# Longer hand-written issue order ahead of attention, and a later start for the pool and LRU branches

## The chip, the cores and the metric

The kernel runs on one core of one Trainium2 chip. The metric is the device time of one execution in microseconds (us); lower is better. Inside a core five engines work beside each other, each with its own instruction queue that is worked off in order: PE (TensorE, matrix products), DVE (VectorE), ACT (ScalarE), POOL (GpSimd) and SP (SyncE, which issues the DMAs here).

## What is computed

Two layers of a hybrid decoder on a sequence of 512 positions with 1024 channels, in float32. Each layer has a mixing part with three parallel branches, merged by sigmoid gates, and a squared-ReLU MLP:

```python
for l in range(DEPTH):                      # 2
    h = rms_norm(x, g_mix[l])
    proj = h @ w_in[l]
    u_pool, q_lat, kv_lat, u_lru, gate_logit = jnp.split(proj, [...], axis=-1)
    y_pool = pool_mixer(u_pool, w_pool_grp[l], pool_scale[l]) @ w_pool_proj[l]
    y_mla = mla_mixer(q_lat, kv_lat, ...) @ w_mla_o[l]      # 8 heads, causal
    y_lru = rg_lru_mixer(u_lru, conv_w[l], ...) @ w_lru_proj[l]
    gates = jax.nn.sigmoid(gate_logit + b_gate[l]).reshape(B, S, N_BRANCH, D)
    merged = gates[:, :, 0] * y_pool + gates[:, :, 1] * y_mla + gates[:, :, 2] * y_lru
    x = x + merged @ w_out[l]
    h = rms_norm(x, g_ffn[l])
    x = x + jnp.square(jax.nn.relu(h @ w_ff1[l])) @ w_ff2[l]
return rms_norm(x, g_final)
```

`pool_mixer` takes causal means over windows of 2, 4, 8 and 16 positions, minus the input, and multiplies each group by a small matrix. `rg_lru_mixer` is a causal convolution of width 4, two small gate products, and a linear recurrence along the sequence.

## The kernel before, in words

Activations lie with channels on the 128 partitions and the 512 positions along the free dimension. Every matrix product is made to float32 accuracy from three products of a high and a low part (`three`): `hi·hi`, `hi·lo`, `lo·hi`. So each weight block of 128x1024 that SP loads (`raw`) is split by ACT (`whi`, a cast, L139) and by DVE (`wlo`, a subtraction, L140); `chunk` does all of that. Two such split blocks and three raw ones fit at a time (`N_W` = 2, `N_RAW` = 3). Activations are split in the same way (`split`, L156 and L157: ACT the high part, DVE or POOL the remainder). `acc` gives one of three PSUM accumulators of 512 columns; a product can begin only when one has been read out.

The mixing part of a layer runs through `mixer` and `merge`:

1. The input projections: the latents for keys and queries, the two LRU blocks and the two pool blocks. This stretch stands in `with tc.manual_schedule(engines=ORDERED)`: inside it PE, DVE and ACT keep the order in which the code is written. It ends with `prefetch(C_V)`, `conv(1)` (the second block's convolution, one multiply at L350 and three multiply-adds at L353, on DVE) and `scaled(project(C_POOL + 1), pm[1])` (L314: DVE reads the last projection out of its accumulator).
2. Outside that block a planner sets the order. It runs a simulation of the engines while it lists instructions: an engine takes, of what is ready, the instruction that comes first in the code. So what is written far behind can be placed early, wherever the simulation sees an engine free. This holds for `windows(0)` and `windows(1)` (the sums of the pool branch on DVE, L364 to L371), for the four products `va` that give the attention's values, and for all that follows.
3. Attention: eight heads, each with score products `s`, a softmax on DVE and ACT (L518 to L524), transposes `t` (L530) and output products `o` (L538). At the heads named in `EARLY` a `gate` is issued: 24 products of 512 columns into `ga`, a multiplication by `rstd` on DVE (L286), a tanh on ACT (L287). There are 24 gates in a layer, three for each of eight output blocks; they keep PE supplied while DVE and ACT work on the softmax.
4. `merge` runs over the 24 gates. At gate `LRU_N` it writes `pool_lru_out`: for each of the two blocks a split of the LRU input and of the pool sums, small products `ra` and `pa`, and a chain of activations up to the recurrence (L571) and a last split. Ahead of that, in layer 0 alone, `setup_vectors` computes small per-channel constants (L260 to L279) that the branch needs. After gate 14 the first merging product `pj` needs the results of all three branches; gates and the convolved LRU inputs share `N_X` = 15 buffers.

`with tc.issue_after(ins)` puts the instructions of its block behind `ins` on the engine of `ins`; `last_gate` holds the last gate's DVE multiplication.

Of the kernel before, what the change touches and what calls it, by code (L numbers as in the profile page):

```python
# [10 lines left out]
F32R = mybir.dt.float32r  # L11
# [4 lines left out]
P = 128  # L16
D = 1024
S = 512
# [16 lines left out]
N_BUSY = 10  # L35
HEAD = 10
SPLIT = 4
EARLY = (0, 2, 4, 6)
LRU_N = 9
DEPTH = 4  # L40
ON_POOL = 2
ORDERED = {mybir.EngineType.PE, mybir.EngineType.DVE, mybir.EngineType.Activation}
# [24 lines left out]
def trunk(ctx: ExitStack, tc, x_in, wts, vecs, consts, out):  # L67
# [66 lines left out]
    def chunk(l, c, cols=1024, off=0):  # L134
        if (l, c) in ready:
            return ready.pop((l, c))
        raw = load(l, c, cols, off)
        hi, lo = wtiles(l, c)
        nc.scalar.copy(hi[:, :cols], raw[:, :cols])  # L139
        nc.vector.tensor_tensor(lo[:, :cols], raw[:, :cols], f(hi[:, :cols]), op=ALU.subtract)  # L140
        return hi, lo
# [139 lines left out]
    def gate(l, rstd, xs, n):  # L281
        j, b = divmod(n, 3)
        a = acc(f"ga{l}_{j}{b}")
        dense(a, chunk(l, C_MIX + 4 * j + b), xs)
        g = xtile(f"g{l}_{j}{b}")
        last_gate[:] = [nc.vector.tensor_tensor(g, a, rstd, op=ALU.mult).ins]  # L286
        nc.scalar.activation(g, g, AF.Tanh, bias=hb[:, l, 4 + 8 * b + j:5 + 8 * b + j], scale=0.5)  # L287
        return g

    def mixer(l, mix, rstd, xs):  # L290
# [3 lines left out]
        with ExitStack() as st:  # L294
# [61 lines left out]
            def windows(b):  # L356

                z, sums = pm[b], []
                cur = z
                for w in (1, 2) if b == 0 else (1, 2, 4, 8):  # L360

                    r = slice(0, P) if len(sums) + 1 < (2 if b == 0 else 4) else slice(64, P)
                    t = xtile(f"win{l}_{b}{w}")
                    nc.vector.tensor_copy(t[r, :w], cur[r, :w])  # L364
                    nc.vector.tensor_tensor(t[r, w:], cur[r, w:], cur[r, :S - w], op=ALU.add)
                    sums.append(t)
                    cur = t
                for r, t in ((slice(0, 64), sums[-2]), (slice(64, P), sums[-1])):
                    cnt = cst[r, K_CNT + 16 * b:K_CNT + 16 * b + 16]
                    nc.vector.tensor_tensor(t[r, 0:16], t[r, 0:16], cnt, op=ALU.mult)  # L370
                    nc.vector.scalar_tensor_tensor(z[r], t[r], cst[r, K_INV + b:K_INV + b + 1], z[r],  # L371
                                                   op0=ALU.mult, op1=ALU.subtract)
# [7 lines left out]
            with tc.manual_schedule(engines=ORDERED):  # L380
# [75 lines left out]
                prefetch(C_V)  # L456
                conv(1)
                scaled(project(C_POOL + 1), pm[1])
            for b in range(2):
                windows(b)  # L460


            wv = chunk(l, C_V)
            v = []
            for t in range(4):
                a = acc(f"va{l}_{t}")
                terms = []
                for k in range(2):
                    h, lo = ckv[k]
                    terms += three(blk(h, t), blk(lo, t), wv[0][:, k * S:(k + 1) * S], wv[1][:, k * S:(k + 1) * S])  # L470
                matmuls(a, terms)
                vv = at.tile([P, NH, 2, DV], F32R, tag="v", bufs=4, name=f"v{l}_{t}")
                split(a.rearrange("p (h d) -> p h d", h=NH), vv[:, :, 0, :], vv[:, :, 1, :])
                v.append(vv)

            pt = [at.tile([P, 13, P], F32R, name=f"pt{l}{c}") for c in "hl"]
            for t in pt:
                nc.vector.memset(f(t[:, 11, :]), 0.0)

            early = []  # L480
            for h in range(NH):
                if h in EARLY:
                    early.append(gate(l, rstd, xs, len(early)))
                e, pr = h % 2, h // 2
# [62 lines left out]
    def pool_lru_out(l, mix, us, pm):  # L547
        w = chunk(l, C_SMALL, 768)
        res = [], []
        for b in range(2):  # L550
            py, ly = (tuple(mix.tile([P, S], F32R, tag="lat", bufs=10, name=f"{n}{c}{l}_{b}") for c in "hl") for n in ("py", "ly"))
            res[0].append(py)
            res[1].append(ly)
            u = us[b]
            split(u, *ly)
            tr, ti = tmp(f"tr{l}_{b}"), tmp(f"ti{l}_{b}")
            for g, t in enumerate((tr, ti)):
                a = acc(f"ra{l}_{b}{g}")
                dense(a, w, [ly], 2 * b + g)
                nc.scalar.activation(t, a, AF.Tanh, bias=hb[:, l, 2 * g + b:2 * g + b + 1], scale=0.5)  # L560

            av, th = tmp(f"av{l}_{b}"), tmp(f"th{l}_{b}")
            sc, ns = sp4[:, l, b:b + 1], nsp4[:, l, b:b + 1]
            nc.scalar.activation(av, tr, AF.Exp, bias=ns, scale=ns)
            nc.scalar.activation(th, tr, AF.Tanh, bias=sc, scale=sc)
            nc.scalar.activation(tr, av, AF.Square)
            nc.vector.scalar_tensor_tensor(th, tr, 1.0, th, op0=ALU.add, op1=ALU.mult)
            nc.scalar.activation(th, th, AF.Sqrt, scale=0.25)
            nc.vector.scalar_tensor_tensor(ti, ti, 1.0, u, op0=ALU.add, op1=ALU.mult)
            nc.vector.tensor_tensor(th, th, ti, op=ALU.mult)  # L570
            nc.vector.tensor_tensor_scan(u, av, th, 0.0, op0=ALU.mult, op1=ALU.add)  # L571
            split(u, *ly)
            split(pm[b], *py)
            a = acc(f"pa{l}_{b}")
            dense(a, w, [py], 4 + b)
            split(a, *py, vcol(l, V_PSC + b))
        return res

    def merge(l, mix, mg, rstd, xs, us, pm, ot, early):
        def project(j, gates):  # L580
            w = chunk(l, C_MIX + 4 * j + 3)
            for b, br, off in ((0, py, 0), (2, ly, 6), (1, ot, 2)):
                a = acc(f"pj{l}_{j}{b}")
                dense(a, w, br, off)
                nc.vector.scalar_tensor_tensor(gates[b], gates[b], 1.0, a, op0=ALU.add, op1=ALU.mult)
                if b:
                    eng = nc.vector if j == KB - 1 else nc.gpsimd
                    eng.tensor_tensor(gates[0], gates[0], gates[b], op=ALU.add)
            h = mg.tile([P, S], F32R, tag="mgh", bufs=KB, name=f"mgh{l}_{j}")
            lo = mg.tile([P, S], F32R, tag="mgl", bufs=KB, name=f"mgl{l}_{j}")  # L590
            split(gates[0], h, lo, 0.5)
            return h, lo

        res = []
        gates = list(early)
        for n in range(3 * KB):
            if n == LRU_N:
                py, ly = pool_lru_out(l, mix, us, pm)
            if n >= len(early):
                gates.append(gate(l, rstd, xs, n))  # L600
            if l == 0 and n == len(early):
                with tc.issue_after(last_gate[0]):
                    setup_vectors()
            j = n // 3 - DEPTH
            if n % 3 == 2 and j >= 0:
                res.append(project(j, gates[3 * j:3 * j + 3]))
        for j in range(KB - DEPTH, KB):
            res.append(project(j, gates[3 * j:3 * j + 3]))
        return res
# [252 lines left out]
```

## Time and profile before

| | us |
|---|---|
| median of 3 runs | 1406.41 (1405.29 to 1406.43) |
| profiled execution, its time | 1406.01 |
| its span, first to last instruction | 1404.1 |
| PE busy | 1382.6 (98% of the span) |
| DVE busy | 780.1 (56%) |
| ACT busy | 559.6 (40%) |
| POOL busy | 257.8 (18%) |

PE is busy nearly throughout, so what is left lies in the few stretches where it waits. Times in rows are counted from the start of the span. Layer 0's mixing part takes about 0 to 352 us, its MLP 352 to 700; layer 1 follows from 700 with the same pattern.

### The profile page before, as it was taken

The numbers are of one execution on the slowest core, as the hardware profiler recorded it, in microseconds if no ns is written. First come the engines' busy times: TensorE is split into PE (matmuls) and PEld (weight loads), VectorE is DVE, ScalarE is ACT, GpSimd is POOL, SyncE is SP. The second block draws the span as 40 slices with busy tenths as digits, with TensorE's granted clock in tenths as the row PEclk, the third lists the DMA queues.
The fourth block names the chain that finished last, engine by engine and source line by source line (L and its number), as shares of the span: only waits on it lengthen the run. The fifth ranks groups of instructions, "written<-read, shape, count | busy, mean of one in ns | idle before, by whom it ended". The sixth has DMA issues, their size and how long they took to land.

```text
span 1404.1 us, 16125 instructions
## 1 busy us (share of the span) xinstructions
PE 1382.6 (98%) x6262; PEld 1145.4 (82%) x6262; DVE 780.1 (56%) x1174; ACT 559.6 (40%) x849; POOL 257.8 (18%) x181
## 2 busy tenths in 40 slices
PE   9999999999999999999999999999999999999997
PEld 7787888888888888888887878888888888888886
DVE  6998875475544324443369987655745433344323
ACT  6467683324422113232344777632343221222322
POOL 0025101033221002211100530111222200022112
PEclk9999999999999999999999999999999999999998
DMA  6221223343333332333332211223423333323231
GB/s 222 88 76 55 68 79 91 102 153 97 99 91 104 90 105 91 100 103 117 123 99 84 77 61 64 91 90 109 147 90 105 93 103 91 104 90 105 91 102 63
DMA packets 42124, 137.38 MB, mean 98 GB/s; under 512 B 4672, under 2 KB 6848, under 8 KB 42048
## 3 DMA queue, kind: packets, MB, share of 16 engines
q1 hardware_dynamic: 41328, 135.76, 30.9%
q8 instruction: 49, 0.80, 0.2%
q10 hardware_dynamic: 720, 0.59, 0.1%
q14 instruction: 27, 0.22, 0.0%
HBM read 132.14 MB, written 4.19 MB: 97 GB/s over the span
## 4 chain that ended last, share of the span: by engine, by line
PE 89%; DVE 7%; ACT 2%; issue 1%; DMA 0%; SPq 0%; DVEq 0%; ACTq 0%
PE f L118 50%; PE ga L118 18%; PE wo L118 6%; PE pj L118 6%; PE in L118 2%; PE s L118 1%; DVE wlo L140 1%; PE o L538 1%; PE t L530 1%; PE qr L118 1%; PE qn L118 1%; PE ka L118 1%; DVE cu L353 1%; DVE p L524 0%; DMA raw<-wts 0%
## 5 line engine op out<-in xcount | busy, mean ns | idle before, releaser
L139 ACT CAST whi<-raw 128x1024 fp32r<-128x1024 f32 (+1 forms) x236 | 246.6, 1045 | 685.1 <-issue 383.2
L140 DVE TENSOR_TENSOR wlo<-raw,whi 128x1024 fp32r<-128x1024 f32 (+1 forms) x236 | 304.0, 1288 | 163.5 <-ACT whi L139 163.5
L118 PE MATMUL f<-al,whi 128*128 128x512 f32 (+1 forms) x528 | 202.2, 383 | 0.0
L118 PE MATMUL f<-ah,whi 128*128 128x512 f32 (+1 forms) x528 | 202.0, 383 | 0.0
L118 PE MATMUL f<-ah,wlo 128*128 128x512 f32 (+1 forms) x528 | 202.0, 383 | 0.0
L118 PE MATMUL f<-xhf,whi 128*128 128x512 f32 x512 | 199.2, 389 | 0.0
L118 PE MATMUL f<-xlf,whi 128*128 128x512 f32 x512 | 199.2, 389 | 0.0
L118 PE MATMUL f<-xhf,wlo 128*128 128x512 f32 x512 | 199.2, 389 | 0.0
L715 POOL TENSOR_TENSOR ft<-ft 128x512 f32<-128x512 f32 x64 | 94.7, 1481 | 426.6 <-ACT ah L714 426.6
L118 PE MATMUL ga<-xhm,whi 128*128 128x512 f32 x384 | 151.8, 395 | 3.1 <-ACT q L501 2.5
L118 PE MATMUL ga<-xhm,wlo 128*128 128x512 f32 x384 | 151.8, 395 | 0.0
L118 PE MATMUL ga<-xlm,whi 128*128 128x512 f32 x384 | 151.2, 394 | 0.0
L118 PEld LDWEIGHTS f<-al,whi 128*128 128x128 f32 x528 | 99.2, 188 | 19.5
L118 PEld LDWEIGHTS f<-ah,whi 128*128 128x128 f32 x528 | 99.2, 188 | 19.4
L118 PEld LDWEIGHTS f<-ah,wlo 128*128 128x128 f32 x528 | 99.2, 188 | 19.3
L118 PEld LDWEIGHTS f<-xlf,whi 128*128 128x128 f32 x512 | 96.1, 188 | 20.0
L118 PEld LDWEIGHTS f<-xhf,whi 128*128 128x128 f32 x512 | 96.1, 188 | 20.0
L118 PEld LDWEIGHTS f<-xhf,wlo 128*128 128x128 f32 x512 | 96.1, 188 | 19.9
L711 DVE SCALAR_TENSOR_TENSOR ft<-f,rstdf 128x512 f32<-128x512 f32 x64 | 44.1, 691 | 102.1 <-PE f L118 102.1
L118 PEld LDWEIGHTS ga<-xhm,whi 128*128 128x128 f32 x384 | 72.8, 189 | 18.2 <-ACT q L501 3.0
L118 PEld LDWEIGHTS ga<-xlm,whi 128*128 128x128 f32 x384 | 72.6, 189 | 14.6
L118 PEld LDWEIGHTS ga<-xhm,wlo 128*128 128x128 f32 x384 | 72.6, 189 | 14.3
(366 smaller groups left out, 2072.4 us busy)
## 6 DMA issues: line engine op xcount, KB each, us to landing
raw<-wts SPq DMA_DIRECT2D x232, 512.0 KB, 3.5
x<-x_in SPq DMA_DIRECT2D x8, 256.0 KB, 5.3
xr<-x_in SPq DMA_DIRECT2D x8, 256.0 KB, 3.1
saved<-xr SPq DMA_DIRECT2D x8, 256.0 KB, 2.0
xr<-saved SPq DMA_DIRECT2D x8, 256.0 KB, 2.8
out<-xr SPq DMA_DIRECT2D x12, 128.0 KB, 1.8
raw<-wts SPq DMA_DIRECT2D x4, 320.0 KB, 2.9
raw<-wts SPq DMA_DIRECT2D x4, 256.0 KB, 5.0
```

The lines of the kernel that those rows point to most:

```text
L118: ins = nc.tensor.matmul(dst, lhsT=a, rhs=b, start=(start and i == 0), stop=(stop and i == n - 1))
L139: nc.scalar.copy(hi[:, :cols], raw[:, :cols])
L140: nc.vector.tensor_tensor(lo[:, :cols], raw[:, :cols], f(hi[:, :cols]), op=ALU.subtract)
L353: nc.vector.scalar_tensor_tensor(u[:, o:], z[:, :S - o], cw(j), u[:, o:], op0=ALU.mult, op1=ALU.add)
L530: nc.tensor.transpose(tp[:, j, :], blk(probs[i], j), ident)
L538: nc.tensor.matmul(o[:, q0 * P:], lhsT=v[j][:, h, :, :], rhs=pt[c][:, 3 * j + q0:3 * j + 4, :], start=(j == 0 and c == 0), stop=(j == 3 an ...
L711: nc.vector.scalar_tensor_tensor(t, a, 0.0, rstd, op0=ALU.max, op1=ALU.mult)
L715: nc.gpsimd.tensor_tensor(t, t, t, op=ALU.mult)
```

## The change

The hand-ordered block goes on: it now also holds the load and split of the first gate's weights, the four products for v with their splits, the load and split of the first query block, `windows(0)` and gate 0. `windows(1)` is written at head 5. The other three early gates stay at heads 2, 4 and 6. `pool_lru_out` is written at gate 11 in place of gate 9, and its first splits (of the LRU input and of the pool sums, both blocks) are put behind the last gate's DVE multiplication and behind its tanh on ACT. `setup_vectors` goes from gate 4 to gate 10.

```diff
-EARLY = (0, 2, 4, 6)
-LRU_N = 9
+EARLY = (2, 4, 6)
+LRU_N = 11
...
-        last_gate[:] = [nc.vector.tensor_tensor(g, a, rstd, op=ALU.mult).ins]
-        nc.scalar.activation(g, g, AF.Tanh, bias=hb[:, l, 4 + 8 * b + j:5 + 8 * b + j], scale=0.5)
+        out = nc.vector.tensor_tensor(g, a, rstd, op=ALU.mult)
+        end = nc.scalar.activation(g, g, AF.Tanh, bias=hb[:, l, 4 + 8 * b + j:5 + 8 * b + j], scale=0.5)
+        last_gate[:] = [out.ins, end.ins]
...
                 scaled(project(C_POOL + 1), pm[1])
-            for b in range(2):
-                windows(b)
-            wv = chunk(l, C_V)
-            v = []
-            for t in range(4):
...
+                prefetch(C_MIX)
+                wv = chunk(l, C_V)
+                v = []
+                for t in range(4):
+                    a = acc(f"va{l}_{t}")
...
+                    split(a.rearrange("p (h d) -> p h d", h=NH), vv[:, :, 0, :], vv[:, :, 1, :])
+                    v.append(vv)
+                ready[l, C_Q] = chunk(l, C_Q, 1024)
+                windows(0)
+                early = [gate(l, rstd, xs, 0)]
...
-            early = []
             for h in range(NH):
+                if h == 5:
+                    windows(1)
                 if h in EARLY:
                     early.append(gate(l, rstd, xs, len(early)))
...
-            split(u, *ly)
+            with tc.issue_after(last_gate[0]), tc.issue_after(last_gate[1]):
+                split(u, *ly)
...
-            split(pm[b], *py)
+            with tc.issue_after(last_gate[0]), tc.issue_after(last_gate[1]):
+                split(pm[b], *py)
...
-            if l == 0 and n == len(early):
+            if l == 0 and n == LRU_N - 1:
                 with tc.issue_after(last_gate[0]):
                     setup_vectors()
```

## Rows read from the trace of the kernel before

**Rows 1.** The page's first part: engine busy us (share of span) xinstructions.
```profile
PE 1382.6 (98%) x6262; PEld 1145.4 (82%) x6262; DVE 780.1 (56%) x1174; ACT 559.6 (40%) x849; POOL 257.8 (18%) x181
```

**Rows 2.** Stretches: start:end, length, busy PE, PEld, DVE, ACT, POOL; clock, DMA, GB/s.
```profile
54.30:72.35 18.05, 14.91 (x63) 11.33 (x63) 17.79 (x30) 6.19 (x10) 0.00 (x0) 1.00 0.29 97
110.00:128.98 18.98, 16.88 (x92) 13.86 (x89) 17.71 (x45) 15.62 (x37) 10.43 (x8) 1.00 0.17 55
128.98:216.26 87.28, 87.28 (x426) 73.31 (x427) 66.65 (x158) 61.52 (x118) 11.98 (x9) 0.98 0.24 72
745.50:764.59 19.09, 17.15 (x68) 13.40 (x67) 18.79 (x32) 5.71 (x8) 0.00 (x0) 0.92 0.30 94
800.00:821.24 21.24, 19.11 (x105) 15.87 (x103) 19.91 (x48) 17.81 (x41) 12.56 (x10) 1.00 0.16 50
```

**Rows 3.** The same view of the two stretches with the clock at half.
```profile
129.92:133.33 3.41, 3.41 (x10) 2.66 (x9) 3.35 (x7) 2.82 (x8) 2.74 (x2) 0.50 0.48 154
761.39:764.80 3.41, 3.41 (x10) 2.66 (x9) 3.28 (x7) 0.59 (x1) 0.00 (x0) 0.50 0.00 0
```

**Rows 4.** Timeline, PE at the v products: start, us, instruction [idle before <-releaser].
```profile
68.76 0.50 PE L118 MATMUL va<-whi,ckvh 128*128 128x512 f32 x1 [1.97 <-DVE v L157]
72.35 0.47 PE L118 MATMUL ga<-xhm,whi 128*128 128x512 f32 x1 [0.53 <-DVE pm L314]
...
760.23 0.50 PE L118 MATMUL va<-whi,ckvh 128*128 128x512 f32 x1 [1.94 <-DVE v L157]
764.59 0.49 PE L118 MATMUL ga<-xhm,whi 128*128 128x512 f32 x1
```

**Rows 5.** Timeline, DVE ahead of and beside the v products.
```profile
55.77 0.54 DVE L350 TENSOR_SCALAR cu<-u,vec 128x512 f32<-128x512 f32 x1
56.35 2.32 DVE L353 SCALAR_TENSOR_TENSOR cu<-u,vec,cu 128x511 f32<-128x511 f32 x3
...
62.99 1.21 DVE L140 TENSOR_TENSOR wlo<-raw,whi 128x1024 fp32r<-128x1024 f32 x1
...
68.03 0.68 DVE L157 TENSOR_TENSOR v<-va,v 128x512 fp32r<-128x512 f32 x1
...
71.53 0.68 DVE L314 TENSOR_TENSOR pm<-in,rstdm 128x512 f32<-128x512 f32 x1
...
754.45 1.22 DVE L140 TENSOR_TENSOR wlo<-raw,whi 128x1024 fp32r<-128x1024 f32 x1
```

**Rows 6.** Timeline, PE in attention, layer 0, where it waits longest.
```profile
127.09 0.63 PE L530 MATMUL t<-cst,p 128*128 128x128 f32 x4 [0.55 <-DVE pt0l L157]
128.98 0.50 PE L118 MATMUL ga<-xhm,whi 128*128 128x512 f32 x1 [1.26 <-ACT q L501]
```

**Rows 7.** Timeline, DVE and ACT, just ahead of those waits.
```profile
123.54 0.68 DVE L157 TENSOR_TENSOR lyl<-cu,lyh 128x512 fp32r<-128x512 f32 x1
...
125.15 0.62 ACT L156 CAST lyh<-cu 128x512 fp32r<-128x512 f32 x1
...
127.74 1.18 ACT L501 COPY q<-qn 64x512 f32<-64x512 f32 x2
```

**Rows 8.** The pool sums' additions, one line's instructions: duration ns min/median/max, first and last start.
```profile
L365 DVE TENSOR_TENSOR win<-win x8: 677/682/683, 67.2 to 769.2; 64x510 f32<-64x510 f32 x2, 128x510 f32<-128x510 f32 x2, 128x508 f32<-128x508 f32 x2, 64x504 f32<-64x504 f32 x2
```

**Rows 9.** The chain that ended last, its piece for the first merging products: start, us, what.
```profile
216.26 5.44 PE pj L118 x24
```

**Rows 10.** Timeline, DVE and ACT: the constants, the LRU branch, gate 10.
```profile
138.10 0.16 DVE L260 COPY lam<-vec 128x2 f32<-128x2 f32 x1
...
152.44 0.17 DVE L279 TENSOR_SCALAR nsp<-sp 128x4 f32<-128x4 f32 x1
...
174.40 0.84 ACT L564 ACTIVATE av<-tr,nsp 128x512 f32<-128x512 f32 x1
...
182.38 1.28 ACT L568 ACT_TABLE_LOAD   x1
...
192.88 0.68 DVE L286 TENSOR_TENSOR g<-ga,rstdm 128x512 f32<-128x512 f32 x1
...
199.29 0.69 DVE L157 TENSOR_TENSOR lyl<-cu,lyh 128x512 fp32r<-128x512 f32 x1
```

More of the change, by code (lines that the diff above doesn't have):

```diff
@@ L458, in mixer @@
                 scaled(project(C_POOL + 1), pm[1])
-            for b in range(2):
-                windows(b)
-            wv = chunk(l, C_V)
-            v = []
-            for t in range(4):
[L466 to L474, printed above, removed]
+                prefetch(C_MIX)
[3 more added lines that the diff above has]
+                    a = acc(f"va{l}_{t}")
+                    terms = []
+                    for k in range(2):
+                        h, lo = ckv[k]
+                        terms += three(blk(h, t), blk(lo, t), wv[0][:, k * S:(k + 1) * S], wv[1][:, k * S:(k + 1) * S])
+                    matmuls(a, terms)
+                    vv = at.tile([P, NH, 2, DV], F32R, tag="v", bufs=4, name=f"v{l}_{t}")
+                    split(a.rearrange("p (h d) -> p h d", h=NH), vv[:, :, 0, :], vv[:, :, 1, :])
[3 more added lines that the diff above has]
+                early = [gate(l, rstd, xs, 0)]
             pt = [at.tile([P, 13, P], F32R, name=f"pt{l}{c}") for c in "hl"]
```

## The prediction

> **What bounds the kernel now.** The page's first part comes first: PE is busy 98% of the span, DVE 56% [rows 1]. A change that leaves the products as they are can only save what PE loses in waits and at half clock, so I looked for the stretches in which PE is not full. The stretches show four, two in each layer. Around the products for v PE is busy 14.91 of 18.05 us in layer 0 and 17.15 of 19.09 in layer 1. Early in attention it is busy 16.88 of 18.98 and 19.11 of 21.24 [rows 2]. In all four DVE is busy 93 to 99%: there DVE sets the pace and PE follows. From 128.98 to the first merging product PE is full and DVE has 20 us to spare [rows 2]. That is the contrast on which everything below rests: DVE work is dear before 129 us and cheap after it.
>
> Then the timeline of PE says what each wait is for. At v, two products run, then PE waits 1.97 us (layer 1: 1.94) for the remainder of the first v, because no accumulator is free; the first gate waits 0.53 more [rows 4]. In attention, transposes wait 0.55 for a remainder on DVE, and a gate 1.26 for ACT to copy a query out of its accumulator [rows 6]. Behind two of the four stretches the clock stands at half, 1.2 GHz, for 3.41 us [rows 3], which costs half of that, 1.7. The wait of 1.97 in layer 0 is not followed by such a fall (clock 1.00 there, [rows 2]), so a fall isn't certain after a wait of this size.
>
> **Part 1: the hand-written order through v and gate 0.** It adds and removes no product. What changes is what stands ahead of the read-outs on DVE. Before, the accumulator of the last pool projection is read at 71.53 [rows 5], although PE had made it, and two v products after it, by 66.8, when its wait of 1.97 began [rows 4]: the convolution's four steps, pool sums and weight splits were dealt in between. In the written order DVE does the low part of v's weights (from 62.99, 1.13 until the next starts), the convolution (2.90, as block 0's from 55.77 to 58.67), then that read-out (0.68) [rows 5]. So the accumulator is free at 62.99 + 4.7 = 67.7 and the third v product starts there in place of 68.76: 1.05 earlier. It ends at 69.3. The fourth needs the first v's remainder: 67.7 + 1.14 (gate weights) + 0.68 = 69.5, so it ends near 70.95; the second remainder is done at 70.1, so gate 0 follows at once, at 70.95 in place of 72.35 [rows 4]. **Gain in layer 0: 1.4.** Waits of about 1.2 stay, since DVE is still behind.
>
> Layer 1 by the same steps: 754.45 [rows 5] + 4.7 = 759.15 for the third product, 1.1 before 760.23; the fourth from 760.95; gate 0 at 762.35 in place of 764.59 [rows 4]: **2.2**. Of this 1.4 is the half clock, which fell on these very products [rows 3]; that it stays away after a wait of 0.9 in place of 1.94 is a guess. If it comes, 0.8 is left, and that is the lower end.
>
> The weight loads and POOL: SP issues the same loads in the same order; gate 1's comes later, as its raw buffer is freed after the low part of gate 0's weights (67.7 + 1.14 = 68.9), and the first query block's weights can be split only when v's products have left theirs. Both lie beside gate 0's own products, 24 x 0.227 = 5.4 on PE [rows 9]. Nothing of POOL's stands in the moved part. ACT gets gate 0's tanh ahead of the first key splits, as before. On DVE, what now queues behind gate 0's read-out is the head work, but that needs products which follow gate 0 on PE. These cost nothing; without that cover the cast and the low part of a weight block would stand on PE's path, some 2.2.
>
> **Part 2: the second pool sums at head 5.** Four shifted additions of 0.68 each [rows 8], with small copies and two closing steps, are some 5 us of DVE per layer. Written at head 5 they only lose precedence: the planner may still place them wherever its simulation sees DVE free, even at 80 us. On DVE that saves between 0 and 5 us before 129. I count 0 for PE by itself, since none of PE's waits of [rows 4, 6] stands directly behind the second sums.
>
> **Part 3: the branch splits behind gate 10.** Before, four pairs of splits stood in the full stretch: on DVE four of 0.68 from 123.54 on, on ACT four of 0.62, two of them at 125.15 and behind, just ahead of the copy at 127.74 that PE waited for [rows 7]. So some 2.5 us goes from either engine ahead of the waits of [rows 6]. PE arrives 1.4 earlier than before, which uses up part of it. Idle time there is 2.1 in either layer [rows 2]. From both sides: all of it may go, 2.1, or none, and as PE comes 1.4 sooner to the same DVE work, the waits may grow by 1.4. I take **1.6 in each layer**: the 1.81 of [rows 6] stands right behind the removed casts, less a little. The half clock at 129.92 [rows 3] follows those waits directly; if they shrink to a few tenths it goes too: **1.7**, or 0.
>
> What the new order adds: the splits now wait behind gate 10's multiplication and tanh, queued on DVE and ACT, and behind them wait the branch's small products, its chain and then the merging products. DVE and ACT have a quarter of that stretch to spare [rows 2]. The 18 small products (18 x 0.227 = 4.1, the spacing from 5.44 for 24 [rows 9]) only change places with gate products on PE. I count 0; the other end is the second rival.
>
> **Sum:** 1.4 + 2.2 + 2 x 1.6 + 1.7 = 8.5. From the profiled execution's 1406.0 that is 1397.5; the median of the runs lies 0.4 above it, so **1397.9 us**. Best case: all idle time and both falls go, 3.1 + 2.1 + 1.7 in layer 0 and 1.9 + 1.7 + 2.1 in layer 1 = 12.6, and some tenths of restart at each wait: 1393.
>
> **Rivals.** *Given back in attention.* DVE's work until 126 is nearly the same sum, so a PE that arrives 1.4 sooner waits 1.4 longer, and the planner deals something else into the gaps. For it: DVE at 93 to 94% there [rows 2]. Against: 2.5 us less on both engines. The gain is then part 1 without part 3, 3.6, less some of its lead: 1403, or 1405 where the clock falls in layer 1 too.
>
> *The LRU branch comes too late (slower).* In layer 0 the constants follow gate 10 as well. Gate 10's read-out stood at 192.88; minus 4.1 for the small products now behind it and 4.7 for what was saved, 184.1. Before, the constants took 138.10 to 152.61 and the branch 174.40 to 199.98 [rows 10], together 14.5 + 25.6 = 40.1, so its last remainder would be there at 224.2. The merging products need it at 216.26 - 4.7 + 1.4 = 213.0 [rows 9]. PE would wait 11.2 and lose another 1.7 by the clock: -8.5 + 12.9 = 4.4 slower, 1410.8. PE waits when the two take over 28.9 us, and the end is slower than before from some 36. Against: before, nobody waited for them and they were dealt out in gaps; 22 steps of 0.16 to 0.2 and a bare chain of some ten steps per block are well under 20 us. The branch changes the activation table four times, 1.28 each [rows 10]. The Trainium skill (ScalarE: Activation LUTs, Rules for kernel authors) says to budget about 2.7 us per change of set; four changes would then add an estimated 5.7 to the chain, and the wait would be 16.9. The row's 1.28 stands against that budget here, so I keep to it.
>
> *Nothing of it arrives.* The planner shifts later work so that other waits appear in the same places: within 2 us of 1406.4.
>
> **Chances.** Forecast 0.54, given back 0.22, late branch 0.16, nothing 0.08. A measurement of this kernel can tell about 0.2%, 2.8 us, from no change. Faster by more than that: the forecast and about half of the first rival, 0.66. Within: 0.20 (the rest of that rival, the last, a branch that is only a little late). Slower: 0.14. The range goes from the best case, 1393, to 1408, which takes in the first rival and a late branch with half its wait.
>
> **What would show it.** Right: gate 0 starts near 71 and 762.4; the wait for v falls below 1.2; no half clock near 130 and 761; no branch split before gate 10; PE's waits between 110 and 129 below 0.6. Wrong: a wait ahead of the first merging product near 211, or ahead of gates 13 and 14, whose buffers the LRU inputs hold; waits for softmax work at new places; a half clock elsewhere.

## The result: 0.7% slower

The changed kernel takes 1415.95 us (median of 4 runs, 1415.66 to 1417.12) beside 1406.12 for the kernel before: ratio 1.0072, 95% interval 1.0055 to 1.009. Forecast were 1397.9 with a range from 1393 to 1408, so the sign was wrong and the time lies outside the range. The profiled execution took 1415.66, its span 1413.5, which is 9.4 more than the span of before. The mean granted clock differs from run to run: single runs of the kernel before lie between 1403.13 us at 0.998 and 1408.67 at 0.994, the changed kernel's four between 1415.66 and 1417.12 at 0.995 or 0.998.

The page of the changed kernel, its busy times and the shares of its chain by engine:

```profile
PE 1383.8 (98%) x6262; PEld 1142.1 (81%) x6262; DVE 784.9 (56%) x1174; ACT 560.5 (40%) x849; POOL 259.9 (18%) x181
...
PE 84%; DVE 11%; ACT 2%; issue 2%; DMA 1%; DVEq 0%; ACTq 0%
```

Beside [rows 1] nothing has happened: the same 6262 products, the same busy time within 1.2 us. The 9.4 us are lost by PE between its products, and a page's shares don't show where. The stretches do. The same view of the changed kernel for v in layer 0, early attention, the end of attention, v in layer 1, the end of attention in layer 1 (columns as in [rows 2]):

```profile
62.72:70.63 7.91, 6.36 (x25) 4.27 (x24) 7.54 (x11) 2.81 (x4) 0.00 (x0) 1.00 0.37 101
70.63:139.60 68.97, 66.42 (x326) 54.85 (x324) 63.62 (x135) 45.45 (x93) 27.45 (x19) 1.00 0.24 73
179.20:221.07 41.87, 36.42 (x168) 28.73 (x167) 30.87 (x67) 32.56 (x52) 3.87 (x3) 1.00 0.17 54
760.12:767.30 7.18, 6.30 (x25) 4.26 (x24) 6.87 (x10) 2.82 (x4) 0.00 (x0) 1.00 0.36 113
875.80:916.00 40.20, 36.22 (x167) 28.65 (x167) 28.09 (x43) 32.41 (x50) 3.86 (x3) 1.00 0.20 65
```

The third and the last row are the news. They are the part that was full before: 128.98 to 216.26 in [rows 2] has no idle time at all, and neither has the same end in layer 1 (kernel before, same view):

```profile
868.20:906.76 38.56, 38.56 (x186) 32.12 (x185) 26.29 (x43) 28.86 (x45) 3.88 (x3) 1.00 0.27 83
```

Now PE stands 5.45 us in it in layer 0 and 3.98 in layer 1. At v the idle time has halved (1.55 and 0.88), and the clock is 1.00 in every stretch of this execution: neither half-clock period of [rows 3] came back.

For comparing many kernels I use one table. For each product of the trace it takes the time from its start to the next product's start, less the usual spacing of its width (0.2263 us for 512 columns, 0.174 for 384, 0.118 for 256, 0.028 for a transpose), and sums this over a stage. So it counts waits, slow restarts and half clock alike; about 1 us per head is always there, from the transposes. The stages are: v (to the start of gate 0), heads 0 to 2, heads 3 to 5, the end (heads 6 and 7 and what follows, up to the first merging product), and pj, the merging products up to the output projection. Layer 0 stands ahead of the stroke, layer 1 behind it; the sum is over the whole kernel. Each row is one execution, the profiled one.

| us lost on PE | v | heads 0-2 | heads 3-5 | end | pj | sum |
|---|---|---|---|---|---|---|
| before | 4.0 / 4.0 | 7.8 / 6.2 | 3.0 / 3.0 | 2.1 / 2.0 | 0.1 / 0.1 | 40.9 |
| after | 2.5 / 1.8 | 7.4 / 7.2 | 3.0 / 3.0 | 9.3 / 7.7 | 0.1 / 0.1 | 50.3 |

The sums differ by 9.4, which is the difference of the spans. The end of attention costs 7.2 + 5.7 = 12.9 more, v 3.7 less. Some of what is lost is half clock and not waiting: where products follow each other without a wait at half clock, their excess spacing is 1.6 of before's 7.8 and 1.5 of its 4.0 at v in layer 1 [rows 3]. The changed kernel has none of it, so its waits and slow restarts alone are some 12.5 more. Half clock has to be taken out of the tables below too before two kernels are compared; its share is given with each.

What PE waits for at that end is in its timeline (changed kernel, the rows with a longer wait; the number in brackets is the idle time ahead of the product, then who ended it):

```profile
185.22 0.30 PE L534 MATMUL t<-cst,p 128*128 128x128 f32 x1 [1.12 <-DVE lam L260]
186.09 0.50 PE L542 MATMUL o<-pt0h,v 128*128 128x512 f32 x1 [0.56 <-ACT pt0h L156]
187.00 0.50 PE L542 MATMUL o<-pt0l,v 128*128 128x512 f32 x1 [0.41 <-DVE pt0l L157]
...
194.01 0.50 PE L542 MATMUL o<-pt0h,v 128*128 128x512 f32 x1 [0.33 <-ACT pt0h L156]
195.30 0.50 PE L118 MATMUL pa<-pyh,whi 128*128 128x512 f32 x1 [0.79 <-DVE pyl L160]
199.17 0.50 PE L118 MATMUL ga<-xhm,whi 128*128 128x512 f32 x1 [1.85 <-DVE pyl L160]
```

Gate 10's last product starts at 183.28, gate 11's first at 199.17. In between PE has only the last two heads' transposes and outputs and the branch's small products, and ahead of them it waits again and again, mostly for a cast or a remainder. (The first row names a copy of a constant, which transposes don't read; a head's remainder ended on DVE just ahead of that copy, at 185.08, and I take that to be what PE waited for.) ACT in the same stretch (changed kernel, timeline):

```profile
183.80 1.04 ACT L139 CAST whi<-raw 128x1024 fp32r<-128x1024 f32 x1
...
185.93 0.72 ACT L287 ACTIVATE g<-g,hb 128x512 f32<-128x512 f32 x1
186.56 0.60 ACT L156 CAST lyh<-cu 128x512 fp32r<-128x512 f32 x1
...
187.18 0.25 ACT L156 CAST pt0h<-t 128x128 fp32r<-128x128 f32 x1
187.32 0.62 ACT L156 CAST pyh<-pm 128x512 fp32r<-128x512 f32 x1
...
187.95 0.61 ACT L156 CAST lyh<-cu 128x512 fp32r<-128x512 f32 x1
188.46 0.62 ACT L156 CAST pyh<-pm 128x512 fp32r<-128x512 f32 x1
...
189.71 0.37 ACT L156 CAST pt0h<-t 128x256 fp32r<-128x256 f32 x1
```

The four casts follow gate 10's tanh at once, as the hold wants it, and the casts `pt0h` that the last heads need stand between them. Note the first row: the high part of gate 11's weights is ready at 184.84, and on DVE the low part at 186.28. So gate 11 didn't wait for its weights. Its first product waits 1.85 for `pyl` (DVE), the instruction that reads the product `pa` out of an accumulator: it waited for one of the three accumulators. DVE rows of the changed kernel (timeline):

```profile
184.53 0.55 DVE L157 TENSOR_TENSOR pt0l<-t,pt0h 128x384 fp32r<-128x384 f32 x1
185.00 0.16 DVE L260 COPY lam<-vec 128x2 f32<-128x2 f32 x1
185.06 1.22 DVE L140 TENSOR_TENSOR wlo<-raw,whi 128x1024 fp32r<-128x1024 f32 x1
```

In this stretch DVE has no room left. From gate 10's last product to gate 11's first, in layers 0 and 1 (changed kernel, columns as above):

```profile
183.67:199.17 15.50, 10.05 (x49) 6.90 (x47) 14.93 (x45) 11.74 (x24) 1.29 (x1) 1.00 0.11 35
880.30:892.90 12.60, 8.62 (x42) 5.97 (x41) 9.77 (x20) 11.90 (x24) 1.27 (x1) 1.00 0.13 42
```

In layer 0 DVE is busy 96% of it, in layer 1, where there are no constants, ACT 94%.

### The profile page after: what moved, and what is told of

Read it like the earlier page. It is cut to its first block, busy times and chain, and to the rows that moved or that the text cites. A ratio compares the mean times of both kernels' runs of the same rounds, so it can differ in the third digit from the quotient of the medians.

```text
span 1413.5 us, 16131 instructions
## 1 busy us (share of the span) xinstructions
PE 1383.8 (98%) x6262; PEld 1142.1 (81%) x6262; DVE 784.9 (56%) x1174; ACT 560.5 (40%) x849; POOL 259.9 (18%) x181
## 4 chain that ended last, share of the span: by engine, by line
PE 84%; DVE 11%; ACT 2%; issue 2%; DMA 1%; DVEq 0%; ACTq 0%
PE f L118 49%; PE ga L118 17%; PE wo L118 6%; PE pj L118 6%; PE in L118 2%; DVE wlo L140 2%; PE s L118 1%; PE o L542 1%; DVE p L528 1%; PE t L534 1%; DVE p L522 1%; DVE cu L354 1%; DVE q L510 0%; DVE pt0l L157 0%; DMA raw<-wts 0%
## 5 line engine op out<-in xcount | busy, mean ns | idle before, releaser
L139 ACT CAST whi<-raw 128x1024 fp32r<-128x1024 f32 x236 | 246.5, 1044 | 680.7 <-issue 374.7
L140 DVE TENSOR_TENSOR wlo<-raw,whi 128x1024 fp32r<-128x1024 f32 x236 | 302.7, 1282 | 162.9 <-ACT whi L139 162.6
```

## The experiments

The kernels stand on two ladders. One starts from the kernel before and adds the hand order (e1), moves the second pool sums (e2, f2, f3, g5), or adds the branch part alone (f4, g2). The other starts from the changed kernel and takes its branch part apart. My theory after the traces: the lost time is made by the late branch (part 3), by a lump of splits at gate 10 and by gates that can't come in between. Rivals: the constants behind gate 10, the second sums, or the longer hand order. Not every expectation came true; what did is said with each group. The medians of before beside which each run stands lie between 1405.7 and 1406.3; ratios are to these, with 95% intervals.

**The hand order alone.** From before: `EARLY` = (2, 4, 6), the block of the diff, `windows(1)` right behind it; `LRU_N` stays 9, splits free, constants at gate 4.

```diff
                 windows(0)
                 early = [gate(l, rstd, xs, 0)]
+            windows(1)
```

> The kernel before with the longer hand order alone (v, first query block, first pool sums and gate 0 in order; the second pool sums written right behind it; LRU branch at gate 9, its splits and the constants free as before). If the changed kernel loses its time behind gate 10 (theory: no gate products left there to fill PE), none of that is here, and only the gain at v is left: gate 0 starts near 70.6, no half clock, some 3.5 us faster than before, 1402 to 1403. Rival, the gain at v is given back as waits in attention: 1405 to 1407.

Measured: 1409.65; 1.0032 (1.0019 to 1.0044), slower than the theory and the rival had it. The gain at v is there (2.5 / 1.8), but heads 0 to 2 lose 11.0 / 10.9, of which 1.6 and 1.5 are half clock. Right behind the block, the second sums now stand ahead of work that PE wants. DVE of this kernel (timeline):

```profile
92.17 0.74 DVE L372 SCALAR_TENSOR_TENSOR pm<-win,cst,pm 64x512 f32<-64x512 f32 x1
...
93.67 0.75 DVE L372 SCALAR_TENSOR_TENSOR pm<-win,cst,pm 64x512 f32<-64x512 f32 x1
94.45 1.23 DVE L140 TENSOR_TENSOR wlo<-raw,whi 128x1024 fp32r<-128x1024 f32 x1
```

PE of the same kernel (timeline):

```profile
95.73 0.50 PE L118 MATMUL ga<-xhm,wlo 128*128 128x512 f32 x1 [1.24 <-DVE wlo L140]
```

The third gate waits 1.24 for a low part that stood behind the sums. Half clock follows at 96.4 (and at 789.3 in layer 1).

**The second sums.** First `windows(1)` at head 5, as in the change; then listed behind attention and put behind gate 4; then the first sums as well; then the first branch splits put behind gate 5:

```diff
 # e2, from e1
+                if h == 5:
+                    windows(1)
 # f2, from e2: in merge, in place of head 5
+            if n == 4:
+                with tc.issue_after(last_gate[0]):
+                    windows(1)
 # g5, from f2
-                windows(0)
...
+                    windows(0)
                     windows(1)
 # f3, from f2: hold = last_gate of gate 5
+            with tc.issue_after(hold[0]), tc.issue_after(hold[1]):
                 split(u, *ly)
```

> The longer hand order and the second pool sums at head 5, but the LRU branch at gate 9 with free splits and the constants at gate 4. Theory (two separate losses: head work of heads 0 and 1 delayed by the second sums on DVE, 1.2 to 2.8 us a layer with the sums at head 5, 1.2 to 7 with the sums right behind the block; and gates lacking at the end of attention, only with the branch at gate 11): the second loss is absent, the first is 2.8 a layer: 1401 to 1403. Rival (the hand order itself costs the time, by PE's earlier arrival): as the hand order alone, 1409 to 1410.

> As e2_block_head5, with the second pool sums written after attention and held behind gate 4 on DVE, so that they can't be placed between heads 0 and 3. Theory (the sums on DVE at 100 to 115 us make PE wait for heads 0 and 1): PE's loss between the first scores and the end of head 1 goes back to 1.2 to 1.6 and 1.6, as before the change: 2 to 5 us faster than e2_block_head5, 1397 to 1400. Rival (PE waits there because it arrives 1.5 to 2 earlier at the same DVE work): within 1 us of e2_block_head5.

> As f2_sums_behind_gate4 (1401.0), with the first pool sums held behind gate 4 too. Theory (DVE work ahead of heads 0 and 1 is what PE waits for): DVE reaches the first heads some 3 us earlier, PE's loss from the first scores to the end of head 2 falls from 5.6 by 0.5 to 2 in each layer: 1397 to 1400. Rival (what is left there is PE's own, transposes and small products): 1400 to 1402.

> As f2_sums_behind_gate4, with the branch's first splits held behind gate 5, so that they leave the stretch of heads 2 and 3 without coming as late as gate 10. Theory (the splits beside heads 2 and 3 cost PE some 1 to 3 us a layer, and a hold harms only where gates have run out): 0 to 4 us faster than f2_sums_behind_gate4, 1395 to 1399. Rival (a hold delays the branch and costs in itself): slower than f2_sums_behind_gate4 by 2 or more.

| | median | ratio | v | heads 0-2 | heads 3-5 | end | sum |
|---|---|---|---|---|---|---|---|
| e2 | 1404.84 | 0.9991 (0.9982 to 1.0) | 2.5 / 1.8 | 7.8 / 7.6 | 3.5 / 3.2 | 2.3 / 2.4 | 39.7 |
| f2 | 1400.97 | 0.9964 (0.9952 to 0.9977) | 2.5 / 1.8 | 5.7 / 5.6 | 3.4 / 3.2 | 2.3 / 2.4 | 35.6 |
| g5 | 1410.26 | 1.0032 (1.002 to 1.0045) | 2.5 / 1.8 | 7.3 / 7.3 | 5.3 / 5.6 | 2.5 / 3.5 | 44.6 |
| f3 | 1405.2 | 0.9994 (0.9985 to 1.0003) | 2.5 / 1.8 | 5.6 / 5.4 | 5.3 / 3.5 | 3.9 / 3.3 | 39.7 |

None of these four traces has half clock in a stage, while 3.1 of before's 40.9 is half clock; so of f2's 5.3 less than before in the sum only 2.2 are waits and restarts, and e2's are 1.9 more than before's. e2 came out slower than expected, f2 1.0 above the range of its theory, f3 as its rival had it, g5 as neither.

"Written at head 5" doesn't mean placed at head 5. DVE of the changed kernel (timeline; in e2 they lie at the same place), first and last step of the second sums:

```profile
100.28 0.67 DVE L366 TENSOR_TENSOR win<-pm 128x511 f32<-128x511 f32 x1
...
113.46 1.34 DVE L372 SCALAR_TENSOR_TENSOR pm<-win,cst,pm 64x512 f32<-64x512 f32 x1
```

The same of f2:

```profile
133.72 0.68 DVE L366 TENSOR_TENSOR win<-pm 128x511 f32<-128x511 f32 x1
...
146.05 0.75 DVE L372 SCALAR_TENSOR_TENSOR pm<-win,cst,pm 64x512 f32<-64x512 f32 x1
```

At head 5 the planner deals them out beside heads 0 and 1, in the stretch in which DVE has nothing to spare (busy 14.33 of the 14.52 us from 100.28 to 114.80). Held behind gate 4 they lie from 133.72 on, and heads 0 to 2 lose 2.1 and 2.0 less. f2 is the best kernel here: 5.3 us below before (1406.23 in its runs), 15 below the changed one. Its stretch up to head 3 and its end (columns as above) show where:

```profile
70.70:135.40 64.70, 63.00 (x314) 52.62 (x314) 58.38 (x125) 46.78 (x96) 26.43 (x19) 1.00 0.23 71
...
179.40:213.00 33.60, 33.57 (x163) 27.65 (x162) 21.87 (x37) 22.97 (x38) 3.51 (x3) 1.00 0.26 85
```

g5 was meant to repeat that gain with the first sums. It lost 9.3 against f2: 4.3 by the table at heads 3 to 5, beside which both sums then lie, 1.3 at the end, and 3.3 at heads 0 to 2, from which DVE work had been taken. So "less DVE work early" is no rule, and I can't say what the planner dealt wrong there. f3 holds the splits to behind gate 5 with the second sums late: heads 0 to 2 stay as they were (5.6 / 5.4), the stages behind lose 4.7, and the kernel 4.2.

**The branch part on the kernel before.** First `LRU_N` = 11 only, then the whole of part 3 (hold behind gate 10, constants at gate 10) without the hand order:

```diff
 # f4
-LRU_N = 9
+LRU_N = 11
 # g2, in addition
+            with tc.issue_after(last_gate[0]), tc.issue_after(last_gate[1]):
                 split(u, *ly)
...
-            if l == 0 and n == len(early):
+            if l == 0 and n == LRU_N - 1:
```

> The kernel before with one number changed: the branch written at gate 11 in place of 9, splits and constants free as before. Theory (writing the branch at gate 11 takes gates 11 and up away as filling for the last two heads): PE loses 3 to 6 us a layer between the end of head 5 and the first merging product, 1411 to 1416. Rival (the loss needs the hold on the splits): within 2 us of before, 1404 to 1408.

> The kernel before with the branch's part of the change alone: written at gate 11, first splits held behind gate 10, constants at gate 10; no longer hand order, pool sums as before. Theory (the hold behind gate 10 puts the splits and small products between gates 10 and 11, where PE has no gates left, and that is the whole of the loss): the loss of the changed kernel at the end of attention, 12 to 13, less what the splits' going saves beside heads 2 and 3 (0 to 3): 1414 to 1419. Rival (the loss needs the hand order, because heads and gates stand otherwise there): 1405 to 1409.

| | median | ratio | v | heads 0-2 | heads 3-5 | end | sum |
|---|---|---|---|---|---|---|---|
| f4 | 1406.51 | 1.0005 (0.9996 to 1.0014) | 4.6 / 3.3 | 6.4 / 7.8 | 3.0 / 3.0 | 2.6 / 2.0 | 41.6 |
| g2 | 1414.43 | 1.0063 (1.005 to 1.0075) | 4.0 / 3.3 | 5.6 / 5.6 | 3.0 / 3.0 | 8.8 / 7.7 | 49.3 |

f4 came out as its rival had it, g2 as its theory. That settles the place: the branch part alone, on the kernel before, makes most of the loss at the end, +6.7 / +5.7. Of that 1.8 in either layer is half clock, so +4.9 / +3.9 are waits and restarts, beside +7.2 / +5.7 in the changed kernel. Writing it two gates later costs nothing clear by itself there (f4). It takes the hold or the constants; the hand order is not needed for it, but these runs don't show that it adds nothing.

**Hold and constants apart.** From the changed kernel: free splits (e3), constants back at gate 4 (e5), both (g3), and the whole behind gate 8 (e4, `LRU_N` = 9).

```diff
 # e3
-            with tc.issue_after(last_gate[0]), tc.issue_after(last_gate[1]):
-                split(u, *ly)
+            split(u, *ly)
 # e5
-            if l == 0 and n == LRU_N - 1:
+            if l == 0 and n == len(early):
 # g3: e3 and e5
 # e4
-LRU_N = 11
+LRU_N = 9
```

> The changed kernel without the hold: the branch's first splits may be placed as early as before, the branch is still written at gate 11. Theory (small products and the last heads stand between gates 10 and 11 without gate products): those still stand there, but run without waiting for splits, so a part comes back, 3 to 6 us: 1410 to 1413. Rival (the hold alone is the loss): all of it, 1401 to 1405.

> The changed kernel with the small constants of layer 0 back at gate 4. Theory (PE has no gate products between gates 10 and 11): layer 1, which has no constants, lost 5.6 us too, so at most the difference between the layers comes back, 1 to 2 us: about 1414. Rival (the constants hold the branch up, as the prediction's slower case had it): most of layer 0's loss goes, 1408 to 1410.

> The changed kernel with free splits and the constants at gate 4; the branch still written at gate 11. It differs from e2_block_head5 (1404.8) by that number alone, and from e3_no_hold (1412.4) by the constants alone. Theory (the writing at gate 11 is harmless by itself, as it was on the kernel before; the hold is what harms): 1404 to 1407, and the constants alone then make the 5 to 8 of e3_no_hold, most of it in layer 0. Rival (the hand order and gate 11 harm together): 1409 to 1412.

> The changed kernel with the branch at gate 9, so that splits and constants are held behind gate 8. Theory (the hold harms where gates are missing behind it; at gate 8 there are score products of heads 6 and 7 as well): half of the loss or less, 1407 to 1411. Rival (only where it stands matters, not the hold): as e2_block_head5, 1404 to 1406.

| | median | ratio | heads 0-2 | heads 3-5 | end | sum |
|---|---|---|---|---|---|---|
| e3 free splits | 1412.36 | 1.0048 (1.0036 to 1.0061) | 7.8 / 7.7 | 2.9 / 2.9 | 9.0 / 3.9 | 47.3 |
| e5 constants at 4 | 1414.46 | 1.0064 (1.0052 to 1.0077) | 7.4 / 7.2 | 3.1 / 3.0 | 7.9 / 8.3 | 50.2 |
| g3 both | 1407.13 | 1.0012 (1.0003 to 1.0021) | 7.8 / 7.7 | 3.0 / 2.9 | 3.3 / 3.9 | 41.8 |
| e4 behind gate 8 | 1416.45 | 1.0075 (1.0061 to 1.0089) | 7.4 / 7.2 | 5.0 / 4.8 | 7.6 / 5.6 | 51.9 |

e3 and e5 came out as their theories had it, g3 just above, e4 slower than theory and rival. Half clock must come out first: it is 1.6 of e3's end in layer 0 and 1.9 / 1.7 of e5's; the changed kernel, g3 and e4 have none. Layer 1 has no constants, and there the end is then 7.7 (changed kernel) or 6.6 (e5) with the hold and 3.9 without (e3, g3). In layer 0 it is 3.3 with neither (g3), 6.0 with the hold alone, 7.4 with the constants alone, 9.3 with both. In the sums, less half clock, the hold costs 4.8 over g3, the constants 3.9, and both together 8.5: they nearly add. The medians (7.3, 5.2 and 8.8 over g3) look as if they didn't, as the falls come in e5 and e3 alone.

Of g3's rest, 2.3 over e2, `LRU_N` = 11 is the only difference; on the kernel before that number cost 0.3 (f4), so writing the branch at gate 11 costs something beside the hand order and the sums at head 5, and nothing clear without them. A hold two gates earlier, with more score products of later heads to fill PE, is no better: part of the loss only moves to heads 3 to 5, and between gate 8's last product and gate 9's first DVE is busy 17.28 of 17.34 us in layer 0.

With the constants late, PE of e3 waits at two products (timeline, layer 0):

```profile
189.94 0.30 PE L534 MATMUL t<-cst,p 128*128 128x128 f32 x1 [1.46 <-DVE pt0l L157]
...
195.79 0.50 PE L542 MATMUL o<-pt0h,v 128*128 128x512 f32 x1 [1.50 <-ACT pt0h L156]
```

Both rows name head work; that the constants, small steps in the same DVE queue from 185 to 199.5, are what held it up is likely and not shown by these rows. ACT of the same kernel waits for the last constant (timeline):

```profile
199.54 0.82 ACT L568 ACTIVATE av<-tr,nsp 128x512 f32<-128x512 f32 x1 [3.80 <-DVE nsp L279]
```

**What holds the hold's loss: accumulators, order, or the lump.** Three edits of the changed kernel. The small products go to the score products' accumulators (e6; h1 with the constants at gate 4). Or the branch is written at gate 13, still held behind gate 10, so that gates 11 and 12 come first (h2, constants at 4). Or only block 1's splits are held (h3, constants at 4).

```diff
 # e6, h1
-                a = acc(f"ra{l}_{b}{g}")
+                a = acc(f"ra{l}_{b}{g}", "s")
...
-            a = acc(f"pa{l}_{b}")
+            a = acc(f"pa{l}_{b}", "s")
 # h2: hold = last_gate of gate 10
-LRU_N = 11
+LRU_N = 13
 # h3, at both places
+            with ExitStack() as held:
+                if b:
+                    for i in last_gate:
+                        held.enter_context(tc.issue_after(i))
                 split(u, *ly)
```

> The changed kernel with the branch's small products (ra, pa) in the two accumulators of the scores, so that the three others stay free for gates. Theory (the small products hold all accumulators, so gate 11 can't fill PE's waits): gates 11 and 12 are dealt in behind gate 10, PE's waits from 184 to 199 and from 881 to 893 go, 8 to 11 us faster than the changed kernel: 1405 to 1408. Rival (the splits come too late, whatever the accumulators): 1413 or more.

> As e6_score_accumulators (1410.6), with the constants at gate 4. Theory (accumulators and missing gates make the loss, the constants 1 to 2 of it in layer 0): 1408 to 1410. Rival (with accumulators free the constants set the end, as the wait of the first merging product there hints): 1404 to 1407.

> As e5_constants_gate4 (1414.5), but the branch is written at gate 13, its splits still held behind gate 10, so that gates 11 and 12 come first in the code and can be dealt in. Theory (PE waits at the end of attention because it has no gate products there): its loss from the end of head 5 to the first merging product falls from 8 to 2 to 4 in each layer, 7 to 11 faster: 1404 to 1407, unless the branch, two gates later still, makes the merging products wait. Rival (the lump of splits on ACT and DVE makes PE wait whatever it has): 1412 to 1415. Rival (the branch comes too late): the loss moves to the first merging products, 1410 or more.

> As e5_constants_gate4 (1414.5), with the hold on the second block's splits alone; the first block's may be placed early. Theory (the first block's products can then be dealt in earlier, and the second's are few): most of the hold's 7.3 goes, 1407 to 1410. Rival (any held split puts the branch's end behind gate 10 and PE waits as before): 1412 to 1415.

| | median | ratio | heads 0-2 | end | pj | sum |
|---|---|---|---|---|---|---|
| e6 | 1410.56 | 1.0036 (1.0022 to 1.005) | 7.4 / 7.2 | 5.2 / 4.2 | 1.9 / 0.6 | 45.2 |
| h1 | 1407.79 | 1.0011 (1.0002 to 1.002) | 7.4 / 7.3 | 3.8 / 4.3 | 0.7 / 0.5 | 43.1 |
| h2 | 1412.45 | 1.0048 (1.0035 to 1.0061) | 7.4 / 7.3 | 3.4 / 2.9 | 2.3 / 4.9 | 46.8 |
| h3 | 1411.42 | 1.0039 (1.0026 to 1.0052) | 7.8 / 7.7 | 6.1 / 6.3 | 0.1 / 0.1 | 46.3 |

The order in which PE's instructions are issued around the end of attention in layer 0, from the programs (`o_6`: head 6, `t_70`: its neighbour's first transposes, `ra_00`: block 0, first gate product; `ga_30`, `ga_31`, `ga_32`: gates 9, 10 and 11; x: how many in a row):

```
before: pa_1x3 ga_30x24 t_62x3 ga_31x2 t_63x4 ga_31x22 ga_32x8 o_6x1 ...
after:  t_62x3 ga_31x2 t_63x4 t_70x1 o_6x8 t_71x2 ra_00x1 ra_01x1 pa_0x1 ...
        ... ra_10x3 ra_11x3 o_7x1 pa_1x3 o_7x7 ga_32x24
e6:     t_63x4 ga_32x2 t_70x1 o_6x1 ga_32x21 o_6x7 t_71x2 ra_00x3 ra_01x3 ...
```

Before, the branch's small products lie ahead of gates 9 to 11, and the gates fill the waits of heads 6 and 7. In the changed kernel all of the branch's 18 small products come out of the hold at once, are listed ahead of gate 11, and hold the three accumulators; gate 11 is issued last. In e6, with other accumulators for them, gate 11 comes where the gap was, 14 us earlier than in the changed kernel. PE of e6 there (timeline):

```profile
185.24 0.50 PE L118 MATMUL ga<-xhm,whi 128*128 128x512 f32 x1 [0.79 <-ACT whi L139]
186.43 0.51 PE L542 MATMUL o<-pt0h,v 128*128 128x512 f32 x1 [0.35 <-ACT pt0h L156]
```

The stretch that is the gap in the changed kernel, in e6 (columns as above):

```profile
183.67:199.17 15.50, 14.15 (x69) 11.07 (x68) 14.56 (x42) 11.44 (x23) 1.29 (x1) 1.00 0.15 41
```

DVE is as full there as in the changed kernel (14.56 beside 14.93), and PE is busy 14.15 in place of 10.05. So a full DVE alone doesn't make PE stand still here; that hangs on the gate that can come in between.

PE of h2 at the merging products of layer 1 (timeline):

```profile
912.38 0.69 PE L118 MATMUL pj<-lyh,whi 128*128 128x512 f32 x1 [2.48 <-ACT lyh L156]
913.45 0.79 PE L118 MATMUL pj<-lyl,whi 128*128 128x512 f32 x1 [0.38 <-DVE lyl L157]
```

e6 came out between theory and rival, h1 just below its theory, h2 as its second rival, h3 between its two. e6 gets 5.1 of 12.9 us back net (sum 50.3 to 45.2, no half clock in either), h1 with the constants early 7.1 beside e5 (50.2 to 43.1), of which 3.6 is e5's half clock. With gates 11 and 12 first (h2) the end is nearer before's (3.4 / 2.9), and now the merging products of layer 1 wait for the branch's last result, 2.48 and 0.38, with half clock behind (912.5). That is the wait of my second rival; that it doesn't appear in the changed kernel because PE has lost its time already is my reading, not shown. h3 shows that half the hold makes less than half of the hold's loss: without half clock e5's end is 6.0 / 6.6, h3's 4.5 / 4.6, g3's 3.3 / 3.9. How much of what e6 leaves at the end (5.2 / 4.2 beside 2.1 / 2.0) is the lump and how much the order can't be told apart by these runs, as each changes the order that the planner deals.

## Why the prediction was wrong

**The reading of what bounds it: right, and too narrow.** DVE sets the pace at v and early in attention. But I took the full stretch behind 128.98 [rows 2] as room in which DVE and ACT work is free. It was full because gates were dealt between the heads' products. The 20 us of DVE were an average over 87 us; the held work came within 15.5, in which DVE was busy 14.93.

**Part 1: right, also in size.** Gate 0 starts at 70.63 (predicted 70.95) in place of 72.35. The v products wait 0.88 and 0.58 and gate 0 not at all, in place of 0.63, 1.97 and 0.53. PE of the changed kernel (timeline), to compare with [rows 4]:

```profile
63.99 0.50 PE L118 MATMUL va<-wlo,ckvh 128*128 128x512 f32 x1 [0.88 <-DVE wlo L140]
...
67.40 0.50 PE L118 MATMUL va<-whi,ckvh 128*128 128x512 f32 x1 [0.58 <-DVE pm L315]
...
70.63 0.39 PE L118 MATMUL ga<-xhm,whi 128*128 128x512 f32 x1
```

The wait of before that [rows 4] leave out:

```profile
64.26 0.50 PE L118 MATMUL va<-wlo,ckvh 128*128 128x512 f32 x1 [0.63 <-DVE wlo L140]
```

The third v product waits for the read-out `pm`, as predicted, and starts at 67.40 (predicted 67.7). By the table v gains 1.5 and 2.2, predicted 1.4 and 2.2. Of layer 1's 2.2 the half clock is 1.5 (1.4 counted). The guess that it would stay away held in every kernel with the block; but in f4 and g2, which lack the block and stand idle 2.5 at that place, it stayed away too, so this part of the agreement may be luck.

**Part 2: the step "I count 0 for PE" failed.** The waits of [rows 4, 6] don't stand behind the second sums of before, because those lie from 73.69 to 82.06, beside gate 0 and the first key and query products. Their first addition and last step there (DVE of the kernel before, timeline):

```profile
73.69 0.68 DVE L365 TENSOR_TENSOR win<-pm 128x511 f32<-128x511 f32 x1
...
81.31 0.75 DVE L371 SCALAR_TENSOR_TENSOR pm<-win,cst,pm 64x512 f32<-64x512 f32 x1
```

Written at head 5 they moved from there, where no such wait stood behind them, to heads 0 and 1. Dealt out there they cost 2 us per layer (e2 to f2). I had written that the planner may place them anywhere, and priced only the saving.

**Part 3: the gain was mis-sized.** Heads 0 to 2 in layer 1, where no half clock disturbs the figure, form a square: with splits and second sums there 7.6 (e2), sums only 7.2 (after), splits only 6.2 (before) or 5.6 (f2, three of the four), neither 5.6 (g2) or 5.4 (f3). So the splits are worth 0.2 to 0.6, not 1.6, and the sums 1.4 to 2. That two casts stand directly ahead of a late copy [rows 7] showed who was last, not what the wait would be without them. In layer 0 the half clock of [rows 3] did go, 1.6 where 1.7 was counted, and the sums that came took most of it back (7.8 to 7.4). What I called "given back in attention" happened here, by the second sums.

**Part 3: "I count 0" for what the later branch adds is the step that decided.** It cost 12.9 us at the end of attention. The kernel with gate 11 and neither hold nor late constants (g3) has 3.1 of that, hold and constants bring the other 9.8. The zero rested on "DVE and ACT have a quarter of that stretch to spare", which holds for the average and not for the 15.5 us in which the work came. I had listed who waits behind the held splits (small products, chain, merging products) and left out the heads: their casts `pt0h` and remainders stand in the same ACT and DVE queues. And 18 small products "only change places with gate products" only if the gates can still come. They came last, for want of an accumulator: with other accumulators for the small products (e6) the end falls from 9.3 / 7.7 to 5.2 / 4.2, 1.8 and 0.5 of which are lost again at the merging products.

The second rival had the sign, less than half of the size (4.4, measured 9.8 by the medians), and not the place: it has PE wait at the merging products, near 211; PE waited from 184 to 199. The constants that it rests on are not needed either, since layer 1 loses 5.7 without them.

**The sum against the result:** predicted -8.5, measured 9.4 by the spans. Part 1 -3.7, predicted -3.6; heads 0 to 2 together 0.6 in place of -4.9; the end 12.9 in place of 0; the other stages -0.4.

**The table loads:** the changed kernel's loads in the branch take 1.28 each too. In these ACT rows of the changed kernel the activation behind the load starts 0.02 after its end, so a change of table costs some 1.3 here. The Trainium skill (ScalarE: Activation LUTs, Rules for kernel authors) budgets about 2.7 us for every switch to a different set; the rows differ from it and decide, as the prediction had it.

```profile
203.08 0.62 ACT L571 ACTIVATE tr<-av 128x512 f32<-128x512 f32 x1
203.72 1.28 ACT L573 ACT_TABLE_LOAD   x1
205.02 0.63 ACT L573 ACTIVATE th<-th 128x512 f32<-128x512 f32 x1
```

## What to carry to other kernels

A stretch in which the bounding engine is full may be full only because filler work is dealt into it. Before work is held back to such a stretch, list for its instructions what queues they enter, how full those are in the few us in which the work will come and not on average, whose buffers they take (here three accumulators), and whether the filler can still come in between. With a planner, the place of a line in the code is a precedence and not a place: what must not run early needs a hold. What a hold is worth has to be measured: for the second sums behind gate 4 it brought 3.9 us (e2 to f2), for the first sums as well it cost 9.3 (g5), for the splits behind gate 5 4.2 (f3), and the hold that released the branch's splits at once behind gate 10 cost more than the rest of the change brought. And compare kernels without their half clock: two falls in one of two traces are worth as much as most edits here.

## What was not expected of the hardware

The clock didn't follow the length of the waits. In the changed kernel's profiled execution PE stood 5.45 us in pieces of up to 1.85 from 184 to 199, 3.98 at the end of layer 1, and the granted clock stayed at 1.00, 2.4 GHz. In g2, e5 and h3, which stand idle less in that stage (3.6 / 3.0, 3.3 / 3.7 and 1.9 / 2.3 us), it fell to half for 3.41 us in both layers: at 186, 188 and 191, and at 883, 891 and 884. So a fall behind a wait, 1.3 to 1.9 us in these traces, is to be carried as a chance, as the prediction did, and a difference of that size between two of these kernels may be a fall and not the edit.
